# Four spare columns in every block of the transposed activations of block 2

## The chip, the cores and the metric

The kernel runs on one core of one Trainium2 chip. The metric is the time of one execution on the device in microseconds (us), taken as the median of several runs; lower is better. Five engines work beside each other: TensorE (PE, matrix products, with its weight loads listed as PEld), VectorE (DVE), ScalarE (ACT), GpSimd (POOL) and SyncE (SP, which issues most of the DMAs).

## The reference, cut to what matters

One sequence of 256 tokens with 1024 features goes through a first block (two mixers and a mixture of 32 experts) and then through two layers of a second block. Everything is float32. The part that the change touches is the second block, whose layers begin every stage with a normalised copy of the activations that is multiplied by a wide matrix of weights:

```
for l in range(DEPTH_2):                                   # 2 layers
    x = x + 0.5 * rmsnorm_2(swiglu(rmsnorm_2(x, ffn1_pre_g[l]), w_ffn1_in[l], w_ffn1_out[l]), ffn1_post_g[l])
    h = rmsnorm_2(x, mix_pre_g[l])
    (z, xbc, dt_raw, rq, rk, rv, rg, aq, ak, av, gate) = jnp.split(h @ w_in[l], offsets, axis=-1)
    ...                                                    # three mixers, gated and added: y
    x = x + rmsnorm_2(y, mix_post_g[l])
    x = x + 0.5 * rmsnorm_2(swiglu(rmsnorm_2(x, ffn2_pre_g[l]), w_ffn2_in[l], w_ffn2_out[l]), ffn2_post_g[l])
```

`w_ffn1_in` and `w_ffn2_in` have 5632 columns each, `w_in` has 10000.

## The kernel before, in words

**Two halves of each number.** A dense product is made of three products in the type fp32r, which the matrix engine takes in one pass: the operand is split into a high part (rounded to fp32r) and a low part (what is left), for the activations (`xTH`, `xTL`) and for the weights (`wh`, `wl`), and high times high, high times low and low times high are added up in PSUM.

**The activations.** `self.xT` (set in `block2`, line 2044) is a pair of tiles of 128 partitions x 8 blocks x 256 tokens. Block k holds features 128k to 128k+127, one per partition, and the 256 tokens along the partition: 256 x 4 = 1024 bytes. `boundary` (the end of every stage) normalises x, transposes it on TensorE, and writes both tiles again: ScalarE the high part, VectorE the low part, 4 blocks x 128 tokens at a time.

**The stream of weights.** Weights come from HBM in chunks of 1 MB by SP's DMAs. A chunk is cut into two units of 8 blocks x 128 columns. ScalarE writes the unit's high part (`wh`), VectorE its low part (`wl`), into rings of four buffers of 4096 bytes per partition each. Line 125 is the wrapper through which every instruction of PE, ACT and DVE is recorded, so nearly all rows of the profile name that line, and they are told apart by their tiles.

**The products.** `wstat` makes one unit's product: for each k, three matmuls, `hv[:, k]` with `H[:, k]`, `hv[:, k]` with `L[:, k]`, `lv[:, k]` with `H[:, k]`. The weights (128 x 128) stand still in the array and 256 columns of `xTH` or `xTL` move through it. A unit is thus 24 matmuls of 128x256, and with the two units of 16 columns there are 302 units, 7248 such matmuls, in block 2. Each has its own weight load. The same routine serves the branch products, where the moving operand is another pair (`yyH`/`yyL`, `yaq`/`yacsB`), and block 1 (`xXH`/`xXL`). In two other places the roles are turned round: in `head_units` and `xstat` a 128 x 128 piece of `xTH` or `xTL` stands still and 512 columns of weights move (384 matmuls), and in the second matrix of a feed-forward stage the pieces that stand still are `fhH`/`fhL`.

**What sets the order.** All engines run an order fixed when the program is built: the work is put out by hand, with the mixers' work slipped between units by `bg`, by counts of estimated time. Engines wait for each other by semaphores alone.

**Where tiles lie.** Pools are stacked in each partition in the order of their opening: `const` first, then the weights' pool, `small`, `gains`, and then `wtsb`, `mo` and block 1's pool `b1` in the first half of the program, or `b2` and a stage's own pool in the second. So a smaller tile in `const` moves all that follows it. `load_vecs` reads small vectors as rows (`col1r`) and transposes them into columns (`col1`); block 1 calls it at line 625.

Of the kernel before, what the change touches and what calls it, by code (L numbers as in the profile page):

```python
# [11 lines left out]
F32R = mybir.dt.float32r  # L12
# [7 lines left out]
T = 256  # L20
NT = 2
D = 1024
KD = 8
# [60 lines left out]
class Parts:  # L84
    """a [128, k, n] operand kept in tiles of four k each"""
# [15 lines left out]
class Counted:  # L101
    """an engine whose instructions add their estimated time (us) to a count of the work handed to it"""
# [37 lines left out]
class Kern:  # L140
# [19 lines left out]
    # ---------------------------------------------------------------- weights  # L160
    def add(self, key, src, shape, dense=True):
        """one chunk of weights: a [128, k, f] load; a dense one is split into units of half its size"""
        i = len(self.chunks)
        k, f = shape
        if not dense:
            parts = None
        elif f <= 256:
            parts = [(0, k, c, min(f, c + 128)) for c in range(0, f, 128)]
        else:
            parts = [(c, c + k // 2, 0, f) for c in (0, k // 2)]  # L170
        self.chunks.append((key, src, shape, parts))
        for n, q in enumerate(parts or ()):
            self.units.append((i, q, n == len(parts) - 1))
# [78 lines left out]
    def get(self, ahead=True):  # L252
        """next unit of the dense stream, (high part, low part)"""
        u = self.n_unit
        self.n_unit += 1
        self.split_to(u)
        if ahead:
            self.ahead(u)
        return self.hl.pop(u)

    def ahead(self, u=None):
        """split what has room: a unit with a place of its own, or a free pair of buffers"""
        self.live = [n for n in self.live if n >= (self.n_unit if u is None else u)]
        while self.n_split != self.limit and (self.n_split in self.place or len(self.live) < self.HL):
            n = self.n_split
            self.split_to(n)
            if self.n_split == n:
                break

    def own(self, pool, tag, width=2048):  # L270
        """a place for both parts of a unit in a tile that nothing else needs by then"""
        def f():
            t = pool.tile([128, width], F32R, name="own", tag=tag, bufs=1)
            return t[:, :1024], t[:, 1024:2048]
        return f

    def expect(self, key):
        """the unit that comes next belongs to this chunk"""
        i = self.units[self.n_unit][0]
        assert self.chunks[i][0] == key, (self.chunks[i][0], key)  # L280
        return sum(1 for n in range(2) if self.n_unit + n < len(self.units) and self.units[self.n_unit + n][0] == i)
# [10 lines left out]
    # ---------------------------------------------------------------- helpers  # L292
# [6 lines left out]
    def wstat(self, key, xT, ps, first=False):  # L299
        """ps columns [j * 256, ...) = (unit j of the chunk)^T xT"""  # L300
        H, L = xT
        nc = self.nc
        for j in range(self.expect(key)):
            hv, lv = self.get()
            m = hv.shape[2]
# [15 lines left out]
    def xstat(self, key, nu, xT, k0, pst, start, stop):  # L321
        """pst[t][half] += xT[:, k0 + k]^T (rows k of the next units)"""
# [3 lines left out]
        for u in range(nu):  # L326
            hv, lv = self.get()
            kk, f = hv.shape[1], hv.shape[2]
# [12 lines left out]
    def xstat_all(self, keys, xT, k0s, po, first=True, tail=3, head=0):  # L341
        """rows of the chunks (two units of one row block each) into po; the last units go token tile by token tile"""
# [24 lines left out]
    def head_units(self, key):  # L367
        """the first 512 columns (of two chunks) against one token tile at a time"""
# [32 lines left out]
    def square(self, out, src):  # L401
        """sum of the squares over 1024"""
# [3 lines left out]
    def msq_end(self, ss):  # L406
        """(mean square + eps) ** -0.5, [128, 1]"""
# [16 lines left out]
    def boundary(self, w, po, gpost, gpre, HL=None, F=None, src=None, r2=None, head=None, rest=None, then=None):  # L424
        """x += po (through gpost * rmsnorm), then w = gpre * rmsnorm(x) and its transpose, split or plain"""
# [156 lines left out]
    def gain(self, ap, scale=1.0, eng=None):  # L582
        """a vector of 1024 on every partition"""
# [6 lines left out]
    def load_vecs(self, pool, items, name):  # L590
        """vectors of 128*n elements as rows, then (vec_cols) as columns [128, n] of one tile"""
# [16 lines left out]
    # ---------------------------------------------------------------- block 1  # L608
# [9 lines left out]
    def block1(self):  # L618
# [6 lines left out]
        vec1 = self.load_vecs(self.cp, [  # L625
# [36 lines left out]
        # ---- c: convolution and silu (twice its value is kept)  # L662
# [36 lines left out]
        # ---- relative bias: rows over the distance, then one shifted row per query  # L699
# [10 lines left out]
        # ---- lambda  # L710
# [58 lines left out]
    def mlstm(self, wmq, wmk):  # L769
# [20 lines left out]
        # ---- gates, their running sums and maxima  # L790
# [7 lines left out]
        # rows of v (with a column of ones)  # L798
# [16 lines left out]
        # running over both chunks: u and M relative to the start cancel where they are used  # L815
        # stacked rows: u at 0, M_in - M at 64, -m at 96
# [14 lines left out]
        # running maxima on every partition  # L831
# [11 lines left out]
        # weight of each key for the state: exp(u - M_end)  # L843
# [196 lines left out]
    def toeplitz_load(self, hk, bd, h0, step):  # L1040
        """hk[p, h, k] = bd[h0 + step * h, p + k] for four rows h"""
# [4 lines left out]
    def toeplitz_mm(self, hk, J, dst, scale=1.0):  # L1046
        """dst[q] = hk[127 - q]"""
# [17 lines left out]
    def band_bias(self, p):  # L1065
        """attention bias of block 2 with its mask, heads in the order (key head, half of the pair, pair)"""
# [19 lines left out]
    def softplus_steps(self, scr, x, n, sign):  # L1086
        """log(1 + exp(sign * x)) on the first n partitions, in steps; the last one yields it"""
# [3 lines left out]
        def lag(n):  # L1091
            """each step waits for the one before"""
            self.load["dve"] += LAG * n
# [25 lines left out]
    # ---------------------------------------------------------------- mixture of experts  # L1119
# [16 lines left out]
    def moe(self):  # L1136
# [11 lines left out]
        # ---- router  # L1148
# [10 lines left out]
        def first_max(src, n, nm):  # L1159
            """value of the maximum and a one-hot of its first place"""  # L1160
# [28 lines left out]
        # ---- place of each token in its experts' lists (1, 2, ...; 0: not of that expert)  # L1189
# [22 lines left out]
        # ---- gates  # L1212
# [38 lines left out]
        for pr in range(16):  # L1251
# [30 lines left out]
            # slots back to tokens, and the gate of each slot  # L1282
# [52 lines left out]
    def overflow(self, gov, flag):  # L1335
        """tokens beyond an expert's slots: every expert on all tokens, weighted by their gates"""
# [39 lines left out]
    # ---------------------------------------------------------------- block 2  # L1376
# [104 lines left out]
    def load_layer(self, l):  # L1481
        """per-channel and per-head parameters of one layer"""
# [38 lines left out]
    def mix(self, l):  # L1521
# [27 lines left out]
        # ---- dt  # L1549
# [5 lines left out]
        # ---- convolution channels  # L1555
# [18 lines left out]
        # ---- attention inputs  # L1574
# [18 lines left out]
        # ---- z and rg through silu (twice its value)  # L1593
# [11 lines left out]
        # ---- retention inputs  # L1605
# [19 lines left out]
        # ---- gates and branches  # L1625
# [50 lines left out]
    def bg(self, force=False):  # L1676
        """work that runs beside the projections: as much as the vector and scalar engines have time for"""
# [30 lines left out]
    def ssd(self):  # L1708
        """plain yield: go on after the next unit of weights; yield 1: go on if there is time"""
# [16 lines left out]
        # running sums: one column per head, and rows for every partition  # L1726
# [105 lines left out]
        # ---- gate and norm  # L1832
# [208 lines left out]
    def block2(self):  # L2041
        nc, a = self.nc, self.a
        self.setup = self.setup2()
        self.xT = (self.b2.tile([128, KD, T], F32R, name="xTH"), self.b2.tile([128, KD, T], F32R, name="xTL"))
        q = self.q = self.b2.tile([128, 8, NT], F32, name="fq")
        with self.tc.tile_pool(name="fin", bufs=1) as p:
# [5 lines left out]
            # x becomes x * gain: the norm's scale comes after, and the next norm's from the scaled squares  # L2052
# [8 lines left out]
            def scale(t):  # L2061
                """r1 = (m + eps) ** -0.5, r1 * r2 = (m2 + eps * (m + eps)) ** -0.5 with m2 of x * gain"""
# [129 lines left out]
```

## Time and profile before

| | us |
|---|---|
| median of three runs | 2200.3 |
| lowest and highest of the three | 2188.7, 2207.75 |
| span of the profiled execution, from its first to its last instruction | 2188.1 |
| TensorE busy in it | 2094.6 (96% of the span) |

The profiled execution's own time is not listed apart from the three runs. The lowest of them, 2188.7, lies 0.6 above its span, and the text takes 2188.7 as its time. The page's second part divides the span into 40 slices of 54.7 us. Block 1 is done by about 125 us, the experts by about 660 us, and the rest of the span is block 2, the part in which `xTH` and `xTL` are used.

How to read it: a matmul's recorded duration includes the time in which the next one already runs, so the pace of a stream of matmuls is read from how far apart they start (the timeline), or from how many fall in a stretch (the view of stretches).

### The profile page before, as it was taken

To read this page: it belongs to the slowest core of one execution; us is meant where nothing else is said; L and a number is where in the kernel's file an instruction comes from. 1 tells how busy PE (TensorE), PEld (TensorE's weight loads), DVE (VectorE), ACT (ScalarE), POOL (GpSimd) and SP (SyncE) were. 2 spreads that over 40 slices of the span, in tenths; PEclk is the share of its full clock that TensorE was granted. 3 is DMA by queue.
4 is the path that set the end of the run, shared out by engine and by line. 5 is a ranking of instruction groups with operands and counts; after the bars stand their busy time and mean duration, and the time that the engine had idled before them with its cause. 6 is when DMAs were issued, how large, how long until landed. Compare 5 with 4: busy or idle time off the path is not lost. (4 is left out here: it accounts for less than half of the span.)

```text
span 2188.1 us, 33683 instructions
## 1 busy us (share of the span) xinstructions
PE 2094.6 (96%) x14031; PEld 1701.1 (78%) x14031; DVE 1107.7 (51%) x1778; ACT 916.0 (42%) x1420; POOL 95.4 (4%) x137
## 2 busy tenths in 40 slices
PE   8979999998897999999999999999999999999998
PEld 7854334333335998999999899889989999997996
DVE  5852011001004655777575655555558775756554
ACT  4441111111014554555644454444446555445442
POOL 3010000000002100000000000010000000001000
PEclk9989999999999999999999999999999999999999
DMA  8389999999997865556247475556546463555652
GB/s 250 122 298 332 375 394 392 396 393 394 397 393 192 227 214 167 168 186 220 89 134 233 145 232 183 193 192 194 194 137 226 137 212 102 167 185 187 218 194 76
DMA packets 316059, 500.05 MB, mean 229 GB/s; under 512 B 11868, under 2 KB 208940, under 8 KB 315392
## 3 DMA queue, kind: packets, MB, share of 16 engines
q1 hardware_dynamic: 309088, 474.88, 63.2%
q0 software_dynamic: 6816, 22.99, 3.6%
q8 instruction: 112, 1.84, 0.3%
q14 instruction: 43, 0.35, 0.0%
HBM read 494.62 MB, written 3.21 MB: 228 GB/s over the span
## 5 line engine op out<-in xcount | busy, mean ns | idle before, releaser
L125 PE MATMUL mm<-xTH,wh 128*128 128x256 f32 x2416 | 679.9, 281 | 0.0
L125 PE MATMUL mm<-xTH,wl 128*128 128x256 f32 x2416 | 672.3, 278 | 3.3 <-DVE wl L125 3.3
L125 PE MATMUL mm<-xTL,wh 128*128 128x256 f32 x2416 | 671.5, 278 | 0.0
L125 DVE TENSOR_TENSOR wl<-raw,wh 128x1024 fp32r<-128x1024 f32 (+1 forms) x380 | 460.2, 1218 | 265.8 <-ACT wh L125 263.8
L125 ACT ACTIVATE wh<-raw 128x1024 fp32r<-128x1024 f32 (+1 forms) x380 | 396.3, 1051 | 212.7 <-PE mm L125 140.1
L125 PEld LDWEIGHTS mm<-xTH,wh 128*128 128x128 f32 x2416 | 454.0, 188 | 6.9 <-issue 5.0
L125 PEld LDWEIGHTS mm<-xTH,wl 128*128 128x128 f32 x2416 | 453.2, 188 | 4.9 <-DVE wl L125 4.3
L125 PEld LDWEIGHTS mm<-xTL,wh 128*128 128x128 f32 x2416 | 452.9, 187 | 2.1 <-issue 1.0
L125 DVE TENSOR_TENSOR hid<-mm,hid 128x512 f32<-128x512 f32 x16 | 11.1, 692 | 289.3 <-PE mm L125 289.3
L125 DVE TENSOR_TENSOR wl<-fraw,wh 128x1024 fp32r<-128x1024 f32 x92 | 112.2, 1225 | 81.7 <-ACT wh L125 81.0
L125 ACT ACTIVATE wh<-fraw 128x1024 fp32r<-128x1024 f32 x92 | 97.1, 1057 | 91.2 <-PE mm L125 48.6
L125 PE MATMUL acc<-wh,fhH 128*128 128x512 f32 x304 | 99.9, 397 | 0.0
L125 PE MATMUL acc<-wh,fhL 128*128 128x512 f32 x304 | 99.7, 396 | 0.0
L125 PE MATMUL acc<-wl,fhH 128*128 128x512 f32 x304 | 99.7, 396 | 0.0
L125 DVE SCALAR_TENSOR_TENSOR yhl<-mm,gs,yhl 128x512 fp32r<-128x512 f32 x32 | 24.0, 751 | 138.4 <-ACT yhl L125 137.3
L125 PE MATMUL mm<-rawB,xg 128*64 128x512 f32 x304 | 82.8, 599 | 2.2 <-DMA rawB<-in_w_eu_dram 2.1
L125 PE MATMUL mm<-raw,xg 128*64 128x512 f32 x264 | 77.6, 597 | 5.0 <-DMA raw<-in_w_eu_dram 4.8
L125 PE MATMUL mm<-yyH,wh 128*128 128x256 f32 x256 | 73.3, 286 | 0.0
L125 PE MATMUL mm<-yyL,wh 128*128 128x256 f32 x256 | 72.1, 282 | 0.0
L125 PE MATMUL mm<-yyH,wl 128*128 128x256 f32 x256 | 72.1, 282 | 0.0
L125 ACT ACTIVATE hidT<-mm 128x512 f32<-128x512 f32 x16 | 9.6, 597 | 146.6 <-PE mm L125 146.6
L125 ACT ACTIVATE yhl<-mm,gs 128x512 fp32r<-128x512 f32 x32 | 22.0, 687 | 115.8 <-PE mm L125 113.8
(532 smaller groups left out, 3326.3 us busy)
## 6 DMA issues: line engine op xcount, KB each, us to landing
raw<-in_w_in_dram SPq DMA_DIRECT2D x88, 1024.0 KB, 5.2
raw<-in_w_ffn_in_dram SPq DMA_DIRECT2D x52, 1024.0 KB, 5.7
fraw<-in_w_ffn_in_dram SPq DMA_DIRECT2D x28, 1024.0 KB, 7.1
raw<-in_w_ffn_out_dram SPq DMA_DIRECT2D x24, 1024.0 KB, 4.9
rawB<-in_w_eg_dram SPq DMA_DIRECT2D x23, 1024.0 KB, 14.6
rawB<-in_w_ed_dram SPq DMA_DIRECT2D x22, 1024.0 KB, 13.8
raw<-in_w_branch_dram SPq DMA_DIRECT2D x22, 1024.0 KB, 5.4
fraw<-in_w_ffn_out_dram SPq DMA_DIRECT2D x20, 1024.0 KB, 5.0
```

The source lines that it names most:

```text
L125: return f(out, *args, **kw)
```

## The change

The diff has two edits; the rest of it takes out comments and docstrings.

```
@@ block1
-        vec1 = self.load_vecs(self.cp, [
+        vec1 = self.load_vecs(p, [
             ("conv_w", a["conv_w"], 16), ("conv_b", a["conv_b"], 4), ("m_norm_g", a["m_norm_g"], 4),
             ("m_skip", a["m_skip"], 4), ("da_norm_g", a["da_norm_g"], 1)], "col1")
...
@@ block2
-        self.xT = (self.b2.tile([128, KD, T], F32R, name="xTH"), self.b2.tile([128, KD, T], F32R, name="xTL"))
+        self.xT = tuple(self.b2.tile([128, KD, T + 4], F32R, name="xT" + n)[:, :, :T] for n in "HL")
```

A block of `xTH` or `xTL` now takes 260 x 4 = 1040 bytes of a partition, of which the first 1024 are used. 1040 is 8 x 128 + 16, so block k starts 16k bytes further on, modulo 128: at 0, 16, 32, 48, 64, 80, 96, 112 where all eight started at 0. The two tiles are 128 bytes longer each. The other edit puts `col1r` and `col1` (512 bytes each) into block 1's pool instead of the constants, which frees 1024 bytes for the whole program. All other tiles of the second half move down by 1024 bytes (the weights' rings and the gains) or 768 (what lies behind `xTL`), both multiples of 128, so that their own places modulo 128 stay:

| tile | byte in the partition before | after | modulo 128, before and after |
|---|---|---|---|
| `xTH` | 95872 | 94848 | 0, and 0 (block 0) |
| `xTL` | 104064 | 103168 | 0, and 0 (block 0) |
| `wh`, `wl` (all four buffers of each; blocks 512 bytes apart) | from 52672, 69056 | from 51648, 68032 | 64 |
| `yyH` / `yyL` | 220864 / 158368 | 220096 / 157600 | 64 / 32 |
| `yaq`, `yacsB` | 166560, 150176 | 165792, 149408 | 32 |
| `fhH`, `fhL` | from 120608 | from 119840 | 32 |
| `own` (weights of the last units of a stage) | e.g. 200480 | 199712 | 32 |

No instruction is added, removed or moved on any engine. One DMA on SP's queue has two more semaphores to wait for, since the tile that it fills (`S`, a buffer for the first experts' weights) now lies where `col1r` and `col1` were. The order of SP's queue around it, before (-) and now (+), `DMASW` being the queue of POOL's DMAs and `DMAHW` that of SP's own:

```order
 L201 DMA gain<-in_w_eg_dram 128x2x512 [waits DMAHW5_49]
 L201 DMA gain<-in_w_eg_dram 128x2x512 [waits DMAHW6_49,DMASW7_49,DVE_49]
-L207 DMA S_1533<-in_w_eg_dram 128x4x512 [waits DMASW5_49,DMASW2_49,DMASW6_49,DMASW1_49,DMAHW7_49,DMASW0_49,Pool_49]
+L207 DMA S_1533<-in_w_eg_dram 128x4x512 [waits DMASW4_49,DMASW3_49,DMASW5_49,DMASW2_49,DMASW6_49,DMASW1_49,DMAHW7_49,DMASW0_49,Pool_49]
 L207 DMA xg<-in_w_eg_dram 128x4x512 [waits DMAHW0_49]
 L207 DMA hT<-in_w_eu_dram 128x4x512 [waits DMAHW1_49,PE_49,Activation_49]
```

Nothing moved there; the two added waits are for small loads on POOL's queue.

## Rows read from the trace of the kernel before

**Rows 1.** The page: busy time of the engines; granted TensorE clock in 40 slices.
```profile
PE 2094.6 (96%) x14031; PEld 1701.1 (78%) x14031; DVE 1107.7 (51%) x1778; ACT 916.0 (42%) x1420; POOL 95.4 (4%) x137
...
PEclk9989999999999999999999999999999999999999
```

**Rows 2.** The page's costliest groups: busy us, mean ns of one, idle time before.
```profile
L125 PE MATMUL mm<-xTH,wh 128*128 128x256 f32 x2416 | 679.9, 281 | 0.0
L125 PE MATMUL mm<-xTH,wl 128*128 128x256 f32 x2416 | 672.3, 278 | 3.3 <-DVE wl L125 3.3
L125 PE MATMUL mm<-xTL,wh 128*128 128x256 f32 x2416 | 671.5, 278 | 0.0
```

**Rows 3.** Chain of work that ended last, one piece: start us, us, what.
```profile
2011.35 106.91 PE mm L125 x938
```

**Rows 4.** Stretches: length; busy us of PE, PEld, DVE, ACT, POOL; clock; DMA; GB/s.
```profile
640.00:2188.00 1548.00, 1515.84 (x11142) 1398.90 (x11138) 951.02 (x1408) 770.65 (x1134) 62.59 (x81) 0.99 0.56 181
1480.00:1550.00 70.00, 70.00 (x620) 70.00 (x619) 39.73 (x39) 33.84 (x40) 0.00 (x0) 1.00 0.60 198
1295.00:1365.00 70.00, 70.00 (x597) 70.00 (x595) 38.97 (x38) 32.97 (x38) 0.00 (x0) 1.00 0.57 185
720.00:800.00 80.00, 80.00 (x681) 80.00 (x681) 46.73 (x50) 40.97 (x47) 5.63 (x10) 1.00 0.80 227
2030.00:2115.00 85.00, 85.00 (x752) 85.00 (x751) 49.74 (x48) 40.52 (x47) 0.00 (x0) 1.00 0.62 201
```

**Rows 5.** Timeline of PE from 916.73: start us, duration us, what.
```profile
916.73 0.36 PE L125 MATMUL mm<-xTH,wh 128*128 128x256 f32 x1
916.93 0.28 PE L125 MATMUL mm<-xTL,wh 128*128 128x256 f32 x1
...
920.89 0.28 PE L125 MATMUL mm<-xTH,wh 128*128 128x256 f32 x1
```

**Rows 6.** Timeline of PE from 1271.99.
```profile
1271.99 0.36 PE L125 MATMUL mm<-xTH,wh 128*128 128x256 f32 x1
1272.19 0.28 PE L125 MATMUL mm<-xTL,wh 128*128 128x256 f32 x1
...
1275.96 0.28 PE L125 MATMUL mm<-xTH,wh 128*128 128x256 f32 x1
```

**Rows 7.** Timeline of PE, a branch product with `yaq` and `yacsB` moving.
```profile
1204.16 0.28 PE L125 MATMUL mm<-yacsB,wh 128*128 128x256 f32 x1
...
1207.83 0.28 PE L125 MATMUL mm<-yaq,wl 128*128 128x256 f32 x1
```

**Rows 8.** Timeline of PE, a branch product with `yyH` and `yyL` moving.
```profile
1073.47 0.28 PE L125 MATMUL mm<-yyL,wh 128*128 128x256 f32 x1
...
1076.09 0.29 PE L125 MATMUL mm<-yyH,wl 128*128 128x256 f32 x1
```

**Rows 9.** Timeline of PE, 512 columns of `own` moving, `fhH` and `fhL` standing.
```profile
868.91 0.39 PE L125 MATMUL acc<-own,fhL 128*128 128x512 f32 x1
...
870.27 0.39 PE L125 MATMUL acc<-own,fhL 128*128 128x512 f32 x1
```

**Rows 10.** Timeline of PE, 512 columns of `own` moving, `xTH` and `xTL` standing.
```profile
883.80 2.04 PE L125 MATMUL mm<-own,xTH 128*128 128x512 f32 x8
885.67 1.10 PE L125 MATMUL mm<-own,xTL 128*128 128x512 f32 x4
```

**Rows 11.** View of tile `xTH`: durations in ns min/median/max, first and last start us.
```profile
L125 PE MATMUL mm<-xTH,wh x2416: 276/276/682, 697.6 to 2117.7; 128*128 128x256 f32 x184, 128*16 128x256 f32 x2
...
L125 ACT ACTIVATE xTH<-mm x24: 592/598/603, 678.5 to 2001.5; 128x512 fp32r<-128x512 f32 x24
L125 DVE TENSOR_TENSOR xTL<-mm,xTH x24: 679/692/693, 679.1 to 2002.1; 128x512 fp32r<-128x512 f32 x24
```

**Rows 12.** Timeline of POOL's issues: the last load of `col1r`.
```profile
10.91 0.52 POOL L596 DMA_DIRECT2D col1r<-in_da_norm_g_dram  x1
```

**Rows 13.** Timeline of SP's issues: the first load into `S`.
```profile
155.59 0.37 SPq L207 DMA_DIRECT2D S<-in_w_eg_dram  x1
```

More of the change, by code (lines that the diff above doesn't have):

```diff
@@ L624, in block1 @@
         self.pump()
-        vec1 = self.load_vecs(self.cp, [
+        vec1 = self.load_vecs(p, [
             ("conv_w", a["conv_w"], 16), ("conv_b", a["conv_b"], 4), ("m_norm_g", a["m_norm_g"], 4),
@@ L2043, in block2 @@
         self.setup = self.setup2()
-        self.xT = (self.b2.tile([128, KD, T], F32R, name="xTH"), self.b2.tile([128, KD, T], F32R, name="xTL"))
+        self.xT = tuple(self.b2.tile([128, KD, T + 4], F32R, name="xT" + n)[:, :, :T] for n in "HL")
         q = self.q = self.b2.tile([128, 8, NT], F32, name="fq")
```

## The prediction

> **What bounds the kernel now.** First the page's busy times and clock: TensorE is busy 96% of the span, VectorE 51%, ScalarE 42%, and the granted clock stands in nine tenths or more in all slices but one [rows 1]. So time is TensorE's, and three groups carry most of it: 7,248 products of 128x256 with `xTH` or `xTL` moving, before which the engine was idle 3.3 us in all [rows 2]. The chain of waits says the same of the end: 106.91 us of matmuls back to back, held by nothing [rows 3].
>
> Then the pace, which the durations (276 to 281 ns) hide, since matmuls overlap. In the stretches that hold nothing else, 70 us from 1480 take 620 matmuls and 70 us from 1295 take 597 [rows 4]. Two or three of each count were running when the stretch began; without them a matmul starts every 113.3 ns in the one and every 117.75 ns in the other. The second pair of stretches gives the same two values: 80 us and 681 matmuls are 117.9 ns, 85 us and 752 are 113.4. In all four the granted clock is 1.00, the 2.4 GHz level, DVE and ACT are busy for 47 to 59% of the time, and DMAs take 0.57 to 0.80. So a dense stream of identical instructions has **two paces**, and neither clock nor a busier neighbour sets them. The two tails of units after an interruption show that a pace, once begun, lasts: both begin with a first interval of 0.20 us, and then 35 intervals take 3.96 us (113.1 ns) in one [rows 5] and 32 take 3.77 us (117.8) in the other [rows 6], with the same operands at the same offsets.
>
> Last, other offsets. Weights stand at 64 modulo 128 in all of these. With `yaq` and `yacsB` moving, both at 32, 31 intervals take 3.67 us, 118.4 ns [rows 7]. With `yyH` at 64 and `yyL` at 32 in turn, 22 take 2.62 us, 119.1 ns [rows 8]. In the 512-column products, moving and standing operand both at 32, 6 intervals take 1.36 us, 226.7 ns [rows 9]; with 32 moving against `xTH` and `xTL` at 0, 8 take 1.87 us, 233.8 [rows 10]. 226.7 is twice 113.3. So the fast pace shows with equal offsets or offsets 64 apart, and offsets 32 apart, or changing inside a unit, show a pace at or above the slow one. That is a handful of pairs; the trace has none 16 or 48 apart.
>
> Over the whole trace the starts of the 7,248 matmuls, the first and last of one third in [rows 11], have 7,102 intervals under 140 ns, 115.05 on average, 62% of them at the fast pace. All at 113.35 would take 7,102 x 1.70 = 12.1 us off the profiled execution (2188.7), giving 2176.6. All at 117.75 would add 19.2, giving 2207.9. The highest of the three runs is 2207.75 and the lowest is the profiled one, so the share of the slow pace alone would explain how the runs differ. The median, 2200.3, is 11.6 above the profiled execution, and stands for a mean of 116.7 ns.
>
> **The change part by part.** *Offsets of the moving blocks.* The instructions stay. In block k the moving operand starts at 16k modulo 128, so its distance from the weights is 64 or 0 in two blocks of eight (k = 0, 4), 32 or 96 in two (k = 2, 6), and 16, 48, 80 or 112 in four, and it changes every third matmul. For the first kind I take what the trace has now as a mixture, 115.05. For the second, 118.4 [rows 7]. The third is not shown; its bounds are the fast pace, 113.35 [rows 4], and the unit with changing offsets, 119.1 [rows 8]. I take 118.4 too, since changing and unequal offsets are nearer to rows 7 and 8 than to any fast row. Mean: (2 x 115.05 + 6 x 118.4) / 8 = 117.56. Against 115.05 that is 2.51 ns x 7,102 = **+17.8 us**. Ends: all 113.35, -12.1 us; all 119.1, +28.8 us.
>
> A rule speaks of this step. The Trainium skill, SBUF — State Buffer, section "Who interferes with whom", says that TensorE and ScalarE never wait for another engine's use of SBUF, and gives the moving operand and the weight load a read port each. The rows agree as far as engines go (the same neighbours at both paces), but two paces for one instruction are more than the page allows for. By the page the offset is worth nothing and the time stays that of the runs.
>
> *Products with `xTH` and `xTL` standing.* 384 of 512 columns. Their weight loads start at 16k instead of 0; moving operands keep 32 or 64. Now 233.8 ns [rows 10], at best 226.7 [rows 9]: at most -2.7 us, and as much the other way if they are at the best place now. I take 0, since rows 10 are already among unequal offsets.
>
> *Writes of the activations.* 24 on ScalarE (598 ns) and 24 on VectorE (692) [rows 11], now with runs 1040 bytes apart. A tenth on each would be 3.1 us, of which only what stands between the stages is on the path. Nothing suggests it; taken as 0, upper end 3.
>
> *Vectors of block 1.* `col1r` and `col1` are written and read by the same instructions. The load into `S` waits for two more loads. The last small load of `col1r` is issued at 10.91 [rows 12], the load into `S` at 155.59 [rows 13], 145 us later, so the waits are over. Were they not, the loads of expert weights queued behind it on SP would be late, with the matmuls that wait for them. Cost 0.
>
> *What follows TensorE.* If its pace slows, splits and weights have more time. If it gains, they must keep up: in the stretch at 113.3 DVE is busy 39.73 of 70 us and ACT 33.84, with no idle time on PE [rows 4]. So a change of the pace reaches the end in full.
>
> Sum: 2188.7 + 17.8 = **2206.5 us**, which is 0.3% above the median 2200.3, though 0.8% above the profiled execution.
>
> **The rivals.** *A, every unit falls into the fast pace.* If the slow pace is a lock that needs the same offset in every block, eight offsets break it, and nothing holds the matmuls above 113.35: 2176.6 us, 1.1% under the median. For it: the slow pace lasts for whole stages, as a lock would. Against: rows 7 and 8, where offsets other than 0 and changing ones are slow too. Chance 0.17.
>
> *B, offsets don't matter.* The two paces remain, drawn anew after each interruption, and rows 7 and 8 have other causes. The time is that of the runs now, 2188.7 to 2207.75, middle 2200. For it: rows 5 and 6, the two paces with all offsets equal. Against: rows 9 and 10, two paces with offsets the only difference that the names show. Chance 0.25.
>
> *C, each new block costs a new wait.* Every third matmul meets a new offset. If each change costs what separates rows 8 from the fast pace (5.8 ns) and the stream never returns to a pace, and the pairs 16 apart are as bad as any, the mean goes to 119.1 and the heads to their upper end: 2188.7 + 28.8 + 2.7 + 3 = 2223 us, 1.0% above the median. It decides against the forecast when the mean interval passes 119. Chance 0.13.
>
> *D, the fast pace itself was a loss from equal offsets.* 256 columns at 2.4 GHz take 106.7 ns, so 6.6 ns per matmul remain even at the fast pace. If a different bank for each block removed a half of them, the mean would be 110: 2188.7 - 5.05 x 7.102 = 2153 us. Against: rows 9 have the same share over twice the columns (226.7 for 213.3), and rows 7 and 8 with other offsets are not below it. Chance 0.03. The Trainium skill, TensorE: Matmul & The Clock Gate, section "Back-to-back issue gap", states about 2.5 ns over the columns' time at full clock; by that figure a matmul would take an estimated 109.2 ns, and no stretch of this trace does.
>
> **How the numbers follow.** The forecast (mixed offsets, 115.5 to 118.7 ns, 2192 to 2218) has 0.42. A measurement of this kernel tells about 1% from no change: under 2178.3 is faster, over 2222.3 slower. Faster: A and D, 0.20. Slower: most of C, with the upper edge of the forecast, 0.13. Within 1%: the rest, 0.67. The range takes in A's 2176.6 and nearly reaches C's 2223: 2176 to 2221, leaving D and the end of C outside.
>
> **What will show it.** In the profile after, the stretch at a stage's dense part (70 us from 1480 or so) should hold about 597 matmuls of `xTH` and `xTL`, not 620, and inside a unit the eight blocks should differ in a pattern that comes back with every unit. 620 everywhere is A, both counts in different stretches is B, 590 or fewer is C, over 630 is D. The rows of `yaq`, `yyH` and `fhH` should stay, as their offsets do, and the chain should still end in matmuls back to back. I am wrong if the pairs 16 apart are at the fast pace: then the mean comes to (6 x 113.35 + 2 x 118.4) / 8 = 114.6, 2185 us.

## The result and the profile after

The kernel with the change takes 2219.93 us (median of 8 runs, 2212.39 to 2223.25), the kernel before in the same session 2198.36 (8 runs, 2188.7 to 2207.75): ratio **1.0091, 95% interval 1.0068 to 1.0113** (the medians alone give 1.0098). The difference of the medians is 21.6 us. The forecast was 2206.5, within 2176 to 2221. Direction and range held, the range by 1.1 us; the time is 13.43 us above the forecast: 9.66 because the sum started from 2188.7 and not from the median (2198.36), and 3.77 because 17.8 us was too little for the change itself.

The profiled execution of after took 2223.25 (span 2221.5), the highest of its eight. That of before is not the 2188.7 that the sum took for it: wherever a time and its span are both listed, the time is 1.7 to 1.9 above the span, so a span of 2188.1 stands for an estimated 2189.9, which is none of the eight and 8.5 under their median. A slow draw is thus set against a quick one, which matters below. TensorE is as busy as in [rows 1], with the same number of instructions:

```profile
PE 2124.9 (96%) x14031; PEld 1732.9 (78%) x14031; DVE 1107.8 (50%) x1778; ACT 915.4 (41%) x1420; POOL 94.9 (4%) x137
...
PEclk9989999999999999999999999999999999999999
...
L125 PE MATMUL mm<-xTH,wh 128*128 128x256 f32 x2416 | 686.8, 284 | 4.7 <-ACT fhid L125 3.9
L125 PE MATMUL mm<-xTH,wl 128*128 128x256 f32 x2416 | 681.3, 282 | 2.7 <-DVE wl L125 2.7
L125 PE MATMUL mm<-xTL,wh 128*128 128x256 f32 x2416 | 679.7, 281 | 0.0
```

VectorE and ScalarE worked as long as before (1107.8 and 915.4 us); TensorE was busy 30.3 us longer over the same 14,031 matmuls. The last dense piece of the chain of waits, the same 938 matmuls as in [rows 3], takes 4.2 us more (start us, us, what):

```profile
2040.47 111.12 PE mm L125 x938
```

The stretches that answer to [rows 4] (length; busy us of PE, PEld, DVE, ACT, POOL; clock; DMA share; GB/s):

```profile
640.00:2221.00 1581.00, 1545.20 (x11157) 1425.97 (x11156) 952.35 (x1410) 770.99 (x1136) 62.17 (x81) 0.99 0.56 178
1499.00:1569.00 70.00, 70.00 (x595) 70.00 (x594) 38.27 (x37) 33.05 (x38) 0.00 (x0) 1.00 0.57 184
1313.00:1383.00 70.00, 70.00 (x595) 70.00 (x594) 38.76 (x38) 32.95 (x38) 0.00 (x0) 1.00 0.56 184
731.00:811.00 80.00, 80.00 (x679) 80.00 (x678) 46.00 (x50) 39.82 (x46) 5.63 (x10) 1.00 0.73 204
2061.00:2146.00 85.00, 85.00 (x722) 85.00 (x721) 47.76 (x46) 39.51 (x46) 0.00 (x0) 1.00 0.57 184
```

Where before had 620 and 597 matmuls in 70 us, after has 595 in both, at the same granted clock of 1.00 (the 2.4 GHz level): the fast pace is gone. Over the trace the 7,063 intervals under 140 ns between starts of `xTH`/`xTL` matmuls average **118.07 ns** (before 115.05, forecast 117.56).

The timeline of PE answers to [rows 7 to 10], and shows the pattern inside the units (start us, duration us, what):

```profile
876.69 0.39 PE L125 MATMUL acc<-own,fhL 128*128 128x512 f32 x1
...
878.05 0.39 PE L125 MATMUL acc<-own,fhL 128*128 128x512 f32 x1
...
885.39 2.03 PE L125 MATMUL mm<-own,xTH 128*128 128x512 f32 x8
887.25 1.08 PE L125 MATMUL mm<-own,xTL 128*128 128x512 f32 x4
...
1087.47 0.28 PE L125 MATMUL mm<-yyL,wh 128*128 128x256 f32 x1
...
1090.08 0.29 PE L125 MATMUL mm<-yyH,wl 128*128 128x256 f32 x1
...
1220.22 0.28 PE L125 MATMUL mm<-yaq,wh 128*128 128x256 f32 x1
...
1223.88 0.28 PE L125 MATMUL mm<-yacsB,wh 128*128 128x256 f32 x1
...
1501.96 0.28 PE L125 MATMUL mm<-xTH,wh 128*128 128x256 f32 x1
...
1504.82 0.28 PE L125 MATMUL mm<-xTH,wh 128*128 128x256 f32 x1
...
1507.63 0.28 PE L125 MATMUL mm<-xTH,wh 128*128 128x256 f32 x1
...
1510.49 0.28 PE L125 MATMUL mm<-xTH,wh 128*128 128x256 f32 x1
...
1513.31 0.28 PE L125 MATMUL mm<-xTH,wh 128*128 128x256 f32 x1
```

What the change did not touch kept its pace: 226.7 ns for `own` with `fhL` (1.36 us for 6), 118.6 for `yyH`/`yyL` (2.61 for 22), 118.1 for `yaq`/`yacsB` (3.66 for 31). `own` against `xTH` went from 233.8 to 232.5 (1.86 for 8). The last five rows are the first matmuls of five units in a row: the units take 2.86, 2.81, 2.86, 2.82 us. The pattern comes back every two units, of 118.9 and 117.5 ns a matmul in turn, all along the stretch.

**A second draw: a late load.** In the first feed-forward stage ScalarE waits for a load of weights (what waited for what: us in total, times, longest). After, then the kernel with `col1` moved alone (the first experiment), then the one with sixteen spare columns (the third):

```profile
ACT wh L125 <- DMA raw<-in_w_ffn_in_dram: 12.7, 1, 12.7
```

```profile
ACT wh L125 <- DMA raw<-in_w_ffn_in_dram: 11.8, 1, 11.8
```

```profile
ACT wh L125 <- DMA raw<-in_w_ffn_in_dram: 5.5, 1, 5.5
```

Of the 14 profiles of this study, seven show one wait of 11.8 us or more there and seven none over 6 (before among these), whatever the offsets. In after TensorE then stands for 5.4 us, and its granted clock is 0.97 from 700 to 750 us (1.00 in before). The first 170 products with `xTH` and `xTL` take 26.8 to 28.8 us in the seven profiles with the late load and 20.1 to 20.9 in the others. After against before is thus a pair with and without it. After against the first experiment is a like pair, both with it: spans 2221.5 and 2197.7, a difference of 23.8 us, of which the pace makes 7,063 x (118.07 - 114.84) = **22.8 us**. So the pace of these matmuls is nearly all of the result.

### The profile page after: what moved, and what is told of

Read it like the earlier page. It is cut to its first block, busy times and chain, and to the rows that moved or that the text cites. A ratio compares the mean times of both kernels' runs of the same rounds, so it can differ in the third digit from the quotient of the medians.

```text
span 2221.5 us, 33684 instructions
## 1 busy us (share of the span) xinstructions
PE 2124.9 (96%) x14031; PEld 1732.9 (78%) x14031; DVE 1107.8 (50%) x1778; ACT 915.4 (41%) x1420; POOL 94.9 (4%) x137
## 5 line engine op out<-in xcount | busy, mean ns | idle before, releaser
L125 PE MATMUL mm<-xTH,wh 128*128 128x256 f32 x2416 | 686.8, 284 | 4.7 <-ACT fhid L125 3.9
L125 PE MATMUL mm<-xTH,wl 128*128 128x256 f32 x2416 | 681.3, 282 | 2.7 <-DVE wl L125 2.7
L125 PE MATMUL mm<-xTL,wh 128*128 128x256 f32 x2416 | 679.7, 281 | 0.0
L125 ACT ACTIVATE wh<-raw 128x1024 fp32r<-128x1024 f32 (+1 forms) x380 | 396.2, 1051 | 227.3 <-PE mm L125 141.2
L125 PEld LDWEIGHTS mm<-xTH,wh 128*128 128x128 f32 x2416 | 454.7, 188 | 11.8 <-issue 4.3
```

What stands on the lines that cost most here:

```text
L125: return f(out, *args, **kw)
```

## The experiments

Each edit is against the changed kernel, whose line is

```
self.xT = tuple(self.b2.tile([128, KD, T + 4], F32R, name="xT" + n)[:, :, :T] for n in "HL")
```

"Place" below is a block's first byte modulo 128, and "distance" how far the moving operand's place is from that of the weights standing in the array; the weights `wh` and `wl` lie at 64 unless said otherwise. Means are of all intervals under 140 ns between starts of `xTH`/`xTL` matmuls.

**1. Padding undone, vectors still moved.**

```
-    ...[128, KD, T + 4], F32R, name="xT" + n)[:, :, :T] for n in "HL")
+    ...[128, KD, T], F32R, name="xT" + n)[:] for n in "HL")
```

> The padding undone, the move of the small vectors (col1) kept: blocks of xTH and xTL again 1024 bytes apart, all at 0 modulo 128. Theory 'place' (a stream of 128x256 matmuls can hold the 113.3 ns pace only while its moving blocks lie at the weights' place modulo 64; elsewhere it runs at about 118) and its rival 'change' (any constant place will do, what breaks the fast pace is that the place changes from block to block): both 0 against the kernel before, 2189 to 2208 us, ratio 0.996 to 1.004, both paces in the trace (mean 114 to 117 ns). Rival 'vectors' (the col1 move and its two added waits on SP's queue carry the loss): about 2215 to 2220, ratio 1.008.

Measured: 2200.76 us, ratio 1.0012 (0.9993 to 1.003), mean 114.84 ns. Both paces are there:

```profile
1292.00:1362.00 70.00, 70.00 (x620) 70.00 (x619) 40.87 (x40) 33.92 (x39) 0.00 (x0) 1.00 0.62 201
...
2036.00:2106.00 70.00, 70.00 (x597) 70.00 (x596) 39.24 (x38) 31.54 (x37) 0.00 (x0) 1.00 0.61 199
```

The move of the vectors and its two added waits cost nothing that can be measured. The loss is the padding's.

**2. All blocks at 32.**

```
+    ...[128, KD * T + 32], F32R, name="xT" + n)[:, 8:8 + KD * T].rearrange("p (k t) -> p k t", k=KD) ...
```

> No spare columns between blocks: all eight blocks of xTH and xTL at 32 modulo 128 (a start 32 bytes later), weights at 64 as before. 'Place': the fast pace is gone everywhere, mean 118.2 ns as for the branch products that always lay at 32, so about 2211 us (2207 to 2218), ratio 1.006 to 1.008. 'Change': the place is constant, so both paces as before, 2189 to 2208, ratio 0.996 to 1.004.

Measured: 2214.29 us, ratio 1.0057 (1.0036 to 1.0079), mean 117.14 ns.

```profile
1297.00:1367.00 70.00, 70.00 (x600) 70.00 (x600) 39.09 (x38) 31.97 (x37) 0.00 (x0) 1.00 0.61 199
```

A place that is constant modulo 128 is not enough: 32 has no fast pace. The size was expected 1 ns too high; `yaq` at the same 32 kept 118.3 ns in this very run, so a place modulo 128 does not fix the pace to the nanosecond (more on this behind experiment 12).

**3. Sixteen spare columns: places 0, 64, 0, 64, ...** (`T + 16`)

> Sixteen spare columns instead of four: blocks 1088 bytes apart, at 0, 64, 0, 64, ... modulo 128. 'Place' (modulo 64): both paces as before, 2189 to 2208 us, ratio 0.996 to 1.004, mean 114 to 117 ns. 'Change': the place changes at each block, so no fast pace, mean near 118, about 2211 to 2220, ratio 1.006 to 1.01. If 128 bytes and not 64 are what counts, this run is slow too and the run at a constant 32 as well.

Measured: 2219.0 us, ratio 1.0095 (1.0071 to 1.0119), mean 118.19 ns.

```profile
1295.00:1365.00 70.00, 70.00 (x594) 70.00 (x593) 38.81 (x38) 31.68 (x37) 0.00 (x0) 1.00 0.60 196
```

"Place modulo 64" falls here: either 64 is itself a bad place, or the alternation is bad. Experiment 5 shows that both are, for blocks at 64 (118.42 ns) and for alternation.

**4. Everything at 0 modulo 64**: `yaq`, `yacsB`, `yyL`, `fhH`, `fhL`, `own` at 64, `yyH` at 0. The padding undone as in 1, and

```
+    self.b2.tile([128, 8], F32, name="pad64")
-        vc = p.tile([128, 2 * NT], F32, name="ssc")
+        vc = p.tile([128, 16], F32, name="ssc")[:, :2 * NT]
```

> No padding; a spare tile of 32 bytes behind xTL and a wider small tile move the stage's own tiles so that yaq, yacsB, yyL, fhH, fhL and own lie at 64 and yyH at 0: every operand of the split products is then at 0 modulo 64, as the weights. 'Place': the branch products (1,128 intervals at 118.5) and the 512-column products (some 1,400 at 232 to 234) get the two paces of xTH and xTL, worth 1,128 x 3.4 ns and 1,400 x about 3.5 ns, some 4 to 9 us: 2185 to 2200, ratio 0.994 to 0.999; if the mixture tips to the fast pace everywhere, 2165. 'Change': the same, where a product's pieces lie at one place; 0 for yaq, which lay at a constant 32.

Measured: 2191.94 us, ratio 0.9976 (0.9959 to 0.9992). The time came out as expected and the reason did not: `yaq` at 64, the weights' own place, got slower (119.6 ns against 118.2), and what gained were 512-column products (ring weights with `fhH`/`fhL` 232.4 against 234.1, `own` with `xT` 231.9 against 233.6). Net of what `yaq` and `own` with `fhH`/`fhL` lost, that is about 1 us of the 6 between the medians; the rest is not accounted for. Something else showed: the `xT` units right behind a branch product, which ran at 113.3 to 113.6 ns in all 18 cases of before, ran at 117.7 to 117.8 in the 12 behind `yyH`/`yyL` (now alternating 0 and 64) and at 113.3 in the 6 behind `yaq` (the first few intervals left out). Where nothing lies between, the stream ahead, with its places, has a say in which pace a stream takes.

**5. Half the blocks at 64.**

```
+    t = [self.b2.tile(s, F32R, name=n) for n, s in (("xTH", [128, 4, T]), ("xTL", [128, 4, T]), ("pad0", [128, 16]),
+         ("xTH1", [128, 4, T]), ("xTL1", [128, 4, T]), ("pad1", [128, 16]))]
+    self.xT = (Parts([t[0], t[3]]), Parts([t[1], t[4]]))
```

> No spare columns; blocks 0 to 3 of xTH and xTL lie at 0 modulo 128, blocks 4 to 7 at 64 (where the weights lie): the same share at each place as with sixteen spare columns (half at 0, half at 64, measured 2219.0 us, 118.19 ns), but one jump inside a unit and one back instead of seven and one. Theory 'place' (each block has the pace of its place, jumps cost nothing): as there, 118.2 ns, 2215 to 2222 us. Theory 'jump' (a place held over several matmuls keeps its pace, a new place at each block costs): blocks at 0 back to the mixture of 113.3 and 117.75 ns (about 115), blocks at 64 near the 119.6 ns that yaq showed when it lay at 64, mean 117.3, about 2213; and 2200 or less if 64 held constant is as good as 0.

Measured: 2212.36 us, ratio 1.0049 (1.0023 to 1.0076), mean 116.73 ns: 115.05 for the blocks at 0, 118.42 for those at 64.

```profile
1298.00:1368.00 70.00, 70.00 (x602) 70.00 (x601) 39.52 (x38) 32.24 (x39) 0.00 (x0) 1.00 0.62 201
```

The same places in the same shares as experiment 3, and 1.46 ns less, 10.4 us over 7,100 matmuls: jumps cost, and what comes back by holding a place is the pace of the blocks at 0, while those at 64 gain nothing. (The medians differ by 6.6; the spans by 2.1, as the profile of 5 has the late load and that of 3 has not.) Inside a unit the first four matmuls at 0 average 120.5, 120.5, 116.3 and 115.0 ns, and the next eight 113.5 to 114.1. A stream needs some four matmuls at distance 64 to reach the fast pace. In the changed kernel a block has three.

**6. Six places, one per stage.**

```
+    t = [self.b2.tile([128, KD * T + 32], F32R, name="xT" + n) for n in "HL"]
+    self.views = [tuple(x[:, o:o + KD * T].rearrange("p (k t) -> p k t", k=KD) for x in t) for o in (4, 12, 16, 20, 24, 28)]
+    self.xT = self.views.pop(0)
...
-    self.boundary(w, po, gpost, gpre, HL=xT, head=head, rest=rest)
+    self.boundary(w, po, gpost, gpre, HL=self.next_xT(), head=head, rest=rest)
```

`next_xT` takes the next of `self.views`.

> No spare columns; within one stage all eight blocks of xTH and xTL lie at one place, but each of the six stages of block 2 has another: 16, 48, 64, 80, 96, 112 modulo 128, in this order (weights at 64). It measures the pace of a constant place. 'Place': each stage shows what the blocks at that place show with four spare columns, 118.3, 117.1, 119.0, 117.6, 118.2, 117.5 ns, within 0.5. 'Jump': the constant places run faster than that, by 0.5 ns or more in the mean, as the constant 32 did (117.14 against 118.6 for the blocks at 32 with four spare columns). Time about 2210 to 2217 us by the first, 2200 to 2212 by the second.

Measured: 2215.76 us, ratio 1.0097 (1.0062 to 1.0132), mean 118.15. The four feed-forward stages (places 16, 64, 80, 112):

```profile
735.00:800.00 65.00, 65.00 (x544) 65.00 (x543) 36.47 (x41) 32.74 (x37) 5.65 (x10) 1.00 0.75 205
1292.00:1362.00 70.00, 70.00 (x596) 70.00 (x596) 39.16 (x38) 31.84 (x37) 0.00 (x0) 1.00 0.61 198
1481.00:1551.00 70.00, 70.00 (x597) 70.00 (x596) 39.24 (x38) 31.91 (x37) 0.00 (x0) 1.00 0.61 197
2051.00:2121.00 70.00, 70.00 (x597) 70.00 (x596) 39.10 (x38) 31.60 (x37) 0.00 (x0) 1.00 0.61 199
```

| place | 0 | 16 | 32 | 48 | 64 | 80 | 96 | 112 | mean |
|---|---|---|---|---|---|---|---|---|---|
| held constant (before, experiments 2 and 6), ns | 115.05 | 119.97 | 117.14 | 117.83 | 117.78 | 117.78 | 118.23 | 117.62 | 117.68 |
| block by block in the changed kernel, ns | 118.41 | 118.33 | 118.61 | 117.09 | 119.02 | 117.55 | 118.20 | 117.46 | 118.08 |

Neither expectation held whole: three of the six places are within 0.5 of "place" (80, 96, 112), and the constant ones are not faster in the mean, as "jump" had it, but 0.26 ns slower. By the table the change costs 3.4 ns at place 0, the one that has a fast pace to lose, and over the other seven it cancels out. That is 0.4 ns in the mean over all eight. What a stage does to the pace and what its place does can't be told apart in this run, and seven of the eight constant places are constant modulo 128 alone: there `xTL` lies 128 bytes from `xTH` modulo 256, at place 0 it does not. So the table doesn't show what a jump by itself costs.

**7. Everything moved by 32 bytes**: `xTH`, `xTL` at 32, weights at 96. The padding undone as in 1, and

```
+    K.cp.tile([128, 8], F32, name="pad32"); K.mhalf = K.cp.tile([128, 8], F32, name="mhalf")
```

> No spare columns; a spare tile of 32 bytes among the constants moves everything behind it: xTH and xTL at 32, weights at 96, yaq, yacsB, yyL, fhH, fhL and own at 64, yyH at 96. All distances between operands are as before, only the places themselves move. If the distance between moving and standing operand decides: as before, 2189 to 2208 us, both paces, mean 114 to 117 ns. If the place of the moving operand itself decides (a row of 1024 bytes that starts at 32 modulo 64): as with all blocks at 32, 117.1 ns, about 2214 (2207 to 2218).

Measured: 2192.37 us, ratio 0.9977 (0.9959 to 0.9994), mean 114.54 ns.

```profile
1281.00:1351.00 70.00, 70.00 (x596) 70.00 (x596) 39.03 (x38) 32.05 (x38) 0.00 (x0) 1.00 0.61 197
1470.00:1540.00 70.00, 70.00 (x620) 70.00 (x620) 40.94 (x40) 33.95 (x40) 0.00 (x0) 1.00 0.63 201
```

Both paces are back at 32. For the one shift tried, the distance between moving and standing operand decides, not the place. Of all distances tried, 64 alone shows the fast pace in 128x256 matmuls.

**8 and 9. Can the pace be set?** One unit in each feed-forward stage, the first behind the interruption, gets tiles of its own (the room of `fhH`/`fhL`'s last part): at distance 0 in 8, at 64 in 9 (`8:8 + 1024`). The padding is undone, and

```
+    fh5 = lambda x: p.tile([128, 1056], F32R, name="fh" + x, tag=f"fh{x}5", bufs=1)
...
+    self.place[self.n_unit + 4] = lambda: [fh5(x)[:, 24:24 + 1024] for x in "HL"]
```

> No spare columns (col1 moved). In each of the four feed-forward stages one unit of weights, the first after the four transposes that interrupt the stream, lies in tiles of its own at 0 modulo 128, where xTH and xTL lie. Theory 'entry' (which of the two paces a stream at distance 64 takes is decided by how it is entered, and a stream at another distance just before always leaves it in the same one, as the 18 xT units that follow a branch product show: all 113.3 to 113.6 ns): the unit itself costs 24 x 6 ns, 0.6 us in all, and the 839 matmuls behind it run at 113.3 to 113.6 ns in all four stages; against the kernel with col1 moved alone (2200.8), where such a stretch is slow about every other time, 4 x 0.5 x 3.7 less 0.6, about 7 us: 2190 to 2196. Rival 'chance': some of the four stretches stay at 117.7, 2198 to 2203.

> The same kernel but for the place of the four units in their own tiles: 64 modulo 128, the distance of all others. 'Entry': nothing is set, the stretches take either pace as before, 2197 to 2204 us. If the gain of the run with the units at 0 came from the extra buffer (a unit split earlier) and not from the place, this one has it as well, 2190 to 2196.

Measured: 2192.01 us, ratio 0.9984 (0.9967 to 1.0002), and 2193.96, ratio 0.9978 (0.9963 to 0.9994). Both have three of the four long stretches at the fast pace. In 8, the unit at distance 0 was followed by

```profile
1280.00:1350.00 70.00, 70.00 (x620) 70.00 (x619) 39.99 (x39) 34.10 (x40) 0.00 (x0) 1.00 0.64 209
1470.00:1540.00 70.00, 70.00 (x596) 70.00 (x595) 39.58 (x38) 33.26 (x38) 0.00 (x0) 1.00 0.54 184
```

One unit does not set the pace, and as the control gained as much, the gain over experiment 1 is not the place's. Whether it is the extra buffer or the draw was not told apart; experiment 7, without the buffer, came out at 2192.4 too.

**10. All stage tiles at distance 64 from the ring weights.** Padding undone, and

```
+    self.b2.tile([128, 24], F32, name="pad96")
+        vc = p.tile([128, 32], F32, name="ssc")[:, :2 * NT]
```

> No spare columns; spare tiles move the stage's own tiles to 0 modulo 128 (yaq, yacsB, yyL, yyH, fhH, fhL, own), so that the branch products and the products of ring weights with fhH and fhL have the distance 64 that xTH and xTL have, while own against xT and against fh has 0. If 64 apart is what gives the two paces: yaq and yy 113 to 118 in place of 118.2 to 118.7, the 512-column products of wh and wl with fh 227 to 235 in place of 234.1; own with xT slower (to 239). Sum about -4 -4 +2 us, 2191 to 2200 against 2200.8. If the branch products' distance was what set the pace of the xT units behind them, those lose their certain 113.3 (18 stretches of 24 to 48 matmuls, up to +2 us).

Measured: 2192.54 us, ratio 0.9981 (0.9967 to 0.9996). Ring weights with `fhH`/`fhL`: 229.96 ns against 234.1. `yaq` and `yy`: 117.84 and 117.76, all at the slow one of the two paces. `own` with `xT`, now at distance 0, did not lose but gained (229.85 against 233.6): the 512-column products have other favourites. The `xT` units behind a branch product ran at 117.7 to 117.8 in 16 of 18 cases. The interleaved stretch of the first mixing stage, before and here:

```profile
1135.00:1220.00 85.00, 85.00 (x733) 85.00 (x732) 53.07 (x58) 41.41 (x53) 0.00 (x0) 1.00 0.57 186
```

```profile
1140.00:1225.00 85.00, 85.00 (x724) 85.00 (x723) 52.29 (x55) 41.19 (x53) 0.00 (x0) 1.00 0.54 180
```

Before, every branch product, at distances 32 and 0, sent the next units off at the fast pace; here the slow pace goes on across products. Why no branch product ran fast at a distance of 64 is taken up behind experiment 12.

**11. Only the feed-forward tiles moved** (padding undone, a tile of 96 bytes first in that pool; the mixers as before).

```
+        p.tile([128, 24], F32, name="pad96")
```

> No spare columns; a spare tile of 96 bytes in the feed-forward stages' pool alone puts fhH, fhL and their own tiles at 0 modulo 128 (64 from the weights), the mixers' tiles stay at 32. By the run with all stage tiles at 0 the 905 products of ring weights with fhH and fhL fall from 234.1 to 230.0 ns (-3.7 us), and the xT units behind a branch product keep the 113.3 to 113.6 ns that they lost there (18 stretches). Theory 'distance 64 and entry': 3 to 5 us under the kernel with col1 moved alone, 2192 to 2197, ratio 0.996 to 0.999. If the 512-column products gain nothing by the distance: 2198 to 2203.

Measured: **2191.47 us, ratio 0.9957 (0.9936 to 0.9978)**, the lowest median here. Products of ring weights with `fhH`/`fhL` took 229.96 ns, and all 18 stretches behind branch products ran at 113.3 to 113.6. The first gives 3.7 us, and `own` with `fhH`/`fhL`, now both at 0, loses 0.5 of it (231.3 ns against 227.4). The interval, 5 to 14 us, is at and above the 3 to 5 expected; what lies beyond is not accounted for.

**12. The same, with two units at 32 in each feed-forward stage.**

```
+        fhx = lambda x, i: p.tile([128, 1056], F32R, name="fh" + x, tag=f"fh{x}{i}", bufs=1)
...
+        for i in range(2):
+            self.place[self.n_unit + 4 + i] = lambda i=i: [fhx(x, 4 + i)[:, 8:1032] for x in "HL"]
```

> The same, and in each feed-forward stage the two units of weights behind the interruption lie in tiles of their own at 32 modulo 128, so that xTH and xTL run 32 bytes off for 48 matmuls, as in the branch products, before they go on at distance 64 for 815. Theory 'entry': 48 matmuls 32 bytes off are enough to leave the stream in the fast pace whatever it was before, so all four stretches at 113.3 to 113.6 ns, for 0.1 to 0.2 us a stage; one unit at distance 0 had been too little (three stretches of four fast, as many as in its control). 2 to 6 us under the run without them, 2187 to 2193. Rival 'chance': one or two of the four stretches stay at 117.7, time as the run without them.

Measured: 2195.31 us, ratio 0.9988 (0.9969 to 1.0006).

```profile
1294.00:1364.00 70.00, 70.00 (x620) 70.00 (x619) 40.84 (x41) 34.20 (x39) 0.00 (x0) 1.00 0.61 198
1480.00:1550.00 70.00, 70.00 (x620) 70.00 (x619) 41.02 (x40) 34.19 (x39) 0.00 (x0) 1.00 0.59 190
2037.00:2107.00 70.00, 70.00 (x620) 70.00 (x619) 40.96 (x40) 33.98 (x39) 0.00 (x0) 1.00 0.61 200
```

In the second, third and fourth stage the stream right behind the two units is fast. In the first it is no test: TensorE stood for 6.95 us behind the two units, for the late load, and ran fast after it until the next interruption, after which 384 matmuls are slow. The runs lie within 5.8 us (2191.77 to 2197.55) where experiment 11's lie within 14. But the median is 3.8 us above experiment 11, against an expected gain (the two intervals overlap a little): the profile of experiment 11 shows the fast pace in the same three long stretches without help, and the 192 matmuls at 32 cost 192 x 5 ns = 1 us. The rest of the 3.8 stays open, and so does why the spread is smaller.

**What modulo 128 leaves open.** Places were counted modulo 128, and no run was made to test that. Modulo 256, `xTH` and `xTL` both start at 128 in before. In the changed kernel `xTL` starts 128 bytes off `xTH`, since a padded tile takes 8320 bytes, which is 32.5 x 256, and so it does in experiments 2 and 6. Three readings say that this counts.

In experiment 5 the two pads move the mixers' tiles by 128 bytes, so that `yaq` and `yacsB` keep their places modulo 128 and not modulo 256. Their 48 matmuls in a row take 5.68 us in experiment 1 (first fence, start us, duration us, what) and 5.76 in experiment 5 (second); the means of all eight such stretches are 118.2 and 119.9 ns. (The units ahead end with blocks at 64 in 5; so they do in experiment 3, where `yaq` kept 118.3.)

```profile
1190.68 0.28 PE L125 MATMUL mm<-yaq,wh 128*128 128x256 f32 x1
...
1196.36 0.28 PE L125 MATMUL mm<-xTH,wh 128*128 128x256 f32 x1
```

```profile
1195.32 0.28 PE L125 MATMUL mm<-yaq,wh 128*128 128x256 f32 x1
...
1201.08 0.28 PE L125 MATMUL mm<-xTH,wh 128*128 128x256 f32 x1
```

In experiment 10 `yaq`, `yacsB` and `yyL` are 64 from the weights modulo 128 but 192 modulo 256, while `xTH` and `xTL` are 64 either way. No branch product ran fast, not even one right behind a fast unit: 15 intervals of `xT` take 1.70 us (113.3 ns), the next 48, of `yyH` and `yyL`, 5.65 us (117.7).

```profile
1030.08 0.28 PE L125 MATMUL mm<-xTH,wh 128*128 128x256 f32 x1
...
1031.78 0.28 PE L125 MATMUL mm<-yyH,wh 128*128 128x256 f32 x1
...
1037.43 0.28 PE L125 MATMUL mm<-xTH,wh 128*128 128x256 f32 x1
```

And of the four units with tiles of their own in experiment 9, whose high and low parts lie 128 bytes apart modulo 256 (a tile of 4224 bytes is 16.5 x 256), three ran at 118.6 to 119.0 ns, which is neither of the two paces. So "distance 64 modulo 128" is not the whole condition. The changed kernel has two things at once, the steps of 16 bytes and the 128 bytes between `xTH` and `xTL`. Experiment 3, whose tiles of 8704 bytes (34 x 256) have no such 128 bytes, shows that steps alone can cost as much; no run has the 128 bytes alone, at place 0.

## Why the prediction was right, and where its sizes were off

**What bounds the kernel**: right. No engine but TensorE mattered, and the pace reached the end in full (22.8 of 23.8 us in the like pair).

**Offsets of the moving blocks**: right in sign and mechanism, +2.51 ns forecast, +3.02 measured, from two errors that partly cancel; that they cancel is luck. For the blocks at 0 and 64 the sum kept the mixture, 115.05; they run at 118.41 and 119.02, an error of 3.67 x 2/8 = +0.92 ns. This is the step that failed: a mixture was taken from streams that stay at one place, but three matmuls are too few to reach the fast pace (experiments 3 and 5), and 64, equal to the weights, never showed it (experiments 4 and 5). For 16, 48, 80, 112, taken at 118.4 for want of a row, the mean is 117.61: -0.79 x 4/8 = -0.40. For 32 and 96, 118.4 was taken from `yaq` and 118.41 measured. Together +0.52 ns, 3.7 us. The step also counted places modulo 128 without a reason; that the padding moves `xTL` by 128 bytes modulo 256 is not in the sum, and its share in the loss stays open. (The trace before has 7,080 such intervals, not 7,102, which is 0.1 us.)

**"The fast pace shows with equal offsets or offsets 64 apart"**: half wrong. For 128x256 matmuls equal offsets are slow (118.4 ns in experiment 5, 119.6 in 4). The evidence, [rows 9], was of 512 columns, where other rules hold, and not even equal offsets settle it: `own` with `fhH`/`fhL` took 227.3 ns with both at 32 in before and 231.3 with both at 0 in experiment 10.

**"The share of the slow pace alone would explain how the runs differ"**: wrong. Experiment 1, profiled at 2199.5 us, had a mean of 114.84, no slower than before's 115.05. Of the 9.6 us between the two spans 6.4 lie in the first 170 products with `xTH` and `xTL`, where its load is late, and 3.1 ahead of them. So the reading of the median as 116.7 ns was wrong too, and with it the base: the forecast stands on the lowest of eight runs. The same +17.8 on the median 2198.4 would have given 2216.2, against the 2219.9 measured. The time thus lies above the 2192 to 2218 of the forecast's own case, although the mean interval, 118.07, lies in its 115.5 to 118.7; the wider range held it by 1.1 us, with some luck.

**Products with `xT` standing, writes, vectors, taken at 0**: right. `own` with `xT` gained 2.0 ns (233.64 to 231.60), the ring weights with `xT` lost some 2.6 (229.4 to 232.1), -0.1 us together. The writes are unchanged, 597 and 691 ns for the 598 and 692 of [rows 11] (view of tile `xTH`: ns min/median/max, first and last start us):

```profile
L125 ACT ACTIVATE xTH<-mm x24: 592/597/601, 683.7 to 2030.6; 128x512 fp32r<-128x512 f32 x24
L125 DVE TENSOR_TENSOR xTL<-mm,xTH x24: 676/691/693, 684.3 to 2031.3; 128x512 fp32r<-128x512 f32 x24
```

The vectors: experiment 1, ratio 1.0012.

**The rivals.** A (all fast) is excluded by 595 matmuls in 70 us. B (offsets don't matter) is excluded by experiments 1 and 2 on one chip: the same instructions, 2200.8 and 2214.3. C named a real effect, a price for each new block: blocks at distance 64 lose the fast pace by it (118.2 ns in experiment 3, 115.05 held for twelve matmuls in experiment 5). The mean stayed under the 119 that C needed. D is excluded: no mean in any run is under 113. The rule weighed with the offsets, from the Trainium skill, SBUF — State Buffer, section "Who interferes with whom", gives the moving operand and the weight load a read port each; read as no effect of addresses, it is contradicted by experiments 2 and 7, in which only addresses differ (117.14 and 114.54 ns).

**The signs named** came: 595 for 597, `yaq`, `yy` and `fh` unmoved, the chain's end in matmuls; the pattern's period is two units, not one.

## What to carry to other kernels

Before padding a matmul operand against conflicts, read the pace from the starts (matmuls per stretch at a granted clock of 1.00) and find its best value and where operands lie when it shows (here modulo 256 at least); padding that steps through all offsets trades one good distance for an average of bad ones. Hold moving and standing operand at the good distance over many matmuls in a row. A sum that starts from one profile should first ask which draws (a late load, a pace) that one execution had.

## What was not expected of the hardware

- Steady paces fall on a grid, though single intervals don't: 113.33 ns is 17 x 6.67, the 120.0 ns that the last four matmuls at 64 of a unit settle on in experiment 5 is 18 x 6.67, and 6.67 ns are 16 cycles at 2.4 GHz. The slow pace repeats after three matmuls (118.3, 117.3, 117.7: together 53 x 6.67), the changed kernel's pattern after two units (5.67 us, 851 x 6.67). These numbers suggest that pace and place lock into cycles; what makes them do so was not tried.
- The stream ahead has a say in a stream's pace: behind the branch products, at distances 32 and 0, it was fast in every case (18 of 18 in before and in each of experiments 1, 7 and 11), behind `yyH`/`yyL` at 0 and 64 it was slow (12 of 12 in experiment 4), behind 48 matmuls 32 bytes off it was fast in the three stages of 12 where nothing lay between, behind 24 at distance 0 in three of four.
- Run to run, the kernel before spreads over 14 to 22 us in its five sets of runs. Two things differ from profile to profile: the pace after an interruption (3.8 us for a stretch of 864 matmuls) and the late load in the first feed-forward stage (about 7 us, in half of the profiles). That they make the whole spread is not shown.
